# A float32 encoder layer on one core: the seven products of a block unit in another order, the fourth one handed on to the next unit

## The chip, the core and the metric

The kernel runs on one core of a Trainium2 chip. Its engines are TensorE (PE in the profile; PEld is its weight load), VectorE (DVE), ScalarE (ACT), GpSimd (POOL) and SyncE (SP). Here SP issues nearly all transfers and POOL the accumulating ones. The metric is the time of one execution in device microseconds.

## What is computed

One layer of a bidirectional encoder on two sequences that share all weights, x_sample (1024 tokens) and x_prompt (512 tokens), D = 2048, float32 throughout. Cut to its products:

```python
def mixer_layer(x, norm_g, w_in, w_dw, b_dw, ln_g, ln_b, w_pw, sink, w_out):
    h = rms_norm(x, norm_g)
    z = h @ w_in                                   # 2048 x 5632
    c_val, c_glu, c_gate, q, k, v, a_gate = jnp.split(z, split_points, axis=-1)
    ...
    conv_out = conformer_conv(c_val, c_glu, w_dw, b_dw, ln_g, ln_b, w_pw) * jax.nn.silu(c_gate)
    attn_out = banded_sink_attention(q, k, v, sink) * jax.nn.silu(a_gate)
    mix = jnp.concatenate([conv_out, attn_out], axis=-1) @ w_out
    return x + mix
```

A final RMS norm follows. The convolution is a depthwise one of 31 taps (on VectorE), the attention is banded over 128-token blocks.

## The kernel before, in words

**Splitting.** A float32 product is made of three passes. Each operand is split into a high part (a copy that is rounded, on ScalarE, L496) and a low part (the difference, on VectorE, L497), and TensorE adds high x high, high x low and low x high. A weight block so needs a raw buffer ("raw", three of 512 KB) and a split buffer ("hl", three).

**Units.** The sample's product with w_in and w_out is cut into units (`Unit`). A unit takes 8 x 128 rows of the contraction and two column tiles of 128 and all 1024 tokens, as a 2 x 2 block product by Winograd's form of Strassen's method: seven products P1 to P7 where eight would be needed. One product is 4 x 3 matmuls of 128 x 128 weights on 512 tokens. Its weight operands are four blocks and three sums of them:

- P1 uses the first column's upper half, P2 its lower half, P3 the second column's lower half;
- P5 uses second upper minus first upper, P6 second lower minus that, P7 second lower minus second upper, P4 first lower minus P6's operand.

The token operands are four blocks and four sums, split once for all units of a stage. The seven products add up in three PSUM banks: `BANK` puts P1, P6, P7 and P4 into bank 0, P2 into bank 1, P5 and P3 into bank 2; `FRESH` products start their bank. After each product a tap (`tap`, L225, in `Onto` L292) reads the bank, and the next product in that bank, which goes on adding, waits until it has been read. A tap writes a tile from `E()`, which hands out tiles of tag g and u in turn (four of each).

**Weights.** A unit has four preps. `load0` (L122) fetches both halves of the first column, `load1` (L126) of the second. `make0` splits the first raw block (for P1 and P2); `make1` makes three sums (L141) and splits P5's and P6's operand; `make2` makes P7's sum and splits it with the second column's lower half (P7 and P3); `make3` splits P4's operand alone. `OPERAND` says which prep and which half of it a product uses. `product` (L185 on) asks for the block it needs, and after its first three matmuls for those up to `look` (three) ahead; `w_prep_now` makes a block and loads those up to three preps on. A block that two products use leaves its hl buffer after the second. In units with `keep`, low parts are also stored for the prompt, and in those with `sums` the three sums, for the last stage.

**Order.** `ALONE` is the order of the seven products in a unit, `TURNS` that in the first pair of units. The first two units of four of the six unit stages are interleaved product by product (`grouped`), the second one in banks of tags s and pt (`side`). `weights_setup` lines up all preps, `run` goes over items (one unit, a pair of units, or a job). The stages are: a unit of plain products, then 7 units (conv columns, first half of the contraction), 8 units (the same, second half, with `total`), 14 and 14 units (the other columns), jobs (`Job`, matmuls L645) for the prompt's input product and the pointwise products, with the attention between, 16 units of `Onto` for w_out, and the prompt's last product (L1781). The unit stages run from 31.7 to 873 us and from 1560 to 1893 us.

**At the seams.** `switch` loads the token sums of the next stage while the last unit of a stage runs and splits them after given products (`unit.after`). `Onto.begin` loads the tile onto which a product is added, `ahead` products early, and `next` hands this on to the next unit. In the last unit of the sample's input products (`end`), `load_two` fetches the prompt's blocks and `follow(step)` splits four of them after product `step`; `end.look` is one less than elsewhere.

**Who waits where.** Instructions of one engine run in the order in which they were put into its queue; the kernel gives weight preps and taps a higher priority (`URGENT`) than the work of its lanes (convolution, attention, preparation), which is doled out as products go by (`tick`).

Of the kernel before, what the change touches and what calls it, by code (L numbers as in the profile page):

```python
# [47 lines left out]
HALF = 4  # L48
# [44 lines left out]
class Unit:  # L93
# [10 lines left out]
    def __init__(self, e, w, cols, k, part, done=None, keep=None):  # L104
        self.e, self.k, self.part, self.done, self.keep = e, k, part, done, keep
        self.total = done is not None
        self.w = [w[c][:, k : k + 2 * HALF, :] for c in cols]
        self.before, self.after, self.d = [], {}, {}
        self.side = False
        self.order = ALONE  # L110
        self.sums = None


# [5 lines left out]

    def load0(self):  # L120
        self.r1 = self.e.raw_tile()
        self.e.nc.sync.dma_start(self.r1, self.w[0])  # L122

    def load1(self):
        self.r2 = self.raw()
        self.e.nc.sync.dma_start(self.r2, self.w[1])  # L126

    late = False
    look = NHL
    STEPS = range(7)  # L130
    landing = LANDING

    def make0(self):
        t = self.e.hl_tile()
        self.e.parts(t[:, 0], t[:, 1], self.r1)
        if self.keep:
            self.e.store(self.keep[0][:, self.k : self.k + 2 * HALF, :], t[:, 1].bitcast(F32).rearrange("p a b c -> p (a b) c"))
        return t

    def sub(self, out, x, y):  # L140
        self.e.nc.vector.tensor_tensor(out, x, y, ALU.subtract)  # L141

    def make1(self):
# [9 lines left out]
        if self.sums:  # L153
            for name, x in (("P5", r1[:, 0]), ("P6", t2), ("P4", r1[:, 1])):
                self.e.store(self.sums[name], x)
        t = self.e.hl_tile()
        for o, x in enumerate((r1[:, 0], t2)):
            self.e.parts(t[:, 0, o], t[:, 1, o], x)
        return t

    def make2(self):
        self.sub(self.r2[:, 0], self.r2[:, 1], self.r2[:, 0])
        if self.sums:
            self.e.store(self.sums["P7"], self.r2[:, 0])
        t = self.e.hl_tile()
        self.e.parts(t[:, 0], t[:, 1], self.r2)
        self.r2 = None
        if self.keep:
            self.e.store(self.keep[1][:, self.k + HALF : self.k + 2 * HALF, :], t[:, 1, 1].bitcast(F32))
        return t  # L170

    def make3(self):
# [6 lines left out]
    def open(self):  # L179
        e = self.e  # L180
        tags = ("s", "s", "pt") if self.side else ("a", "b", "c")
        self.bank = [None] * 3
        self.tags = tags

    def product(self, step, late):  # L185
        e, nc = self.e, self.e.nc
        name = self.order[step]
        p, o = OPERAND[name]
        i = self.at[p]
        e.w_prep(i + 1)  # L190
        hl = e.hl[i]
        n = BANK[name]
        if name in FRESH:
            self.bank[n] = e.PS(self.tags[n], [W])
        acc = self.bank[n]
        toks = e.T[SUMS[name]]
        for j in range(HALF):
            for q, (l, r) in enumerate(((0, 0), (0, 1), (1, 0))):
                nc.tensor.matmul(  # L199
                    acc,  # L200
                    hl[:, l, o, j, :],
                    toks[j][:, r],
                    start=name in FRESH and j == 0 and q == 0,
                    stop=name in LAST and j == HALF - 1 and q == 2,
                    skip_group_check=True,
                )
# [52 lines left out]
class Onto(Unit):  # L259
# [5 lines left out]

    def __init__(self, e, w, cols, k, source, part, done=None):
        super().__init__(e, w, cols, k, part, done)
        self.source, self.next, self.ahead = source, None, 1

    def begin(self, n):  # L270
        if n not in self.d:
            self.d[n] = self.e.E()
            self.e.nc.sync.dma_start(self.d[n], self.source(*n))

    def open(self):
        super().open()
        self.begin((0, 0))

    def product(self, step, late):
        step_of = step + self.ahead  # L280
        if step_of < len(self.order):
            name = self.order[step_of]
            if name in self.START:
                self.begin(self.START[name])
        elif self.next:
            self.next.begin((0, 0))
        return super().product(step, late)

    def tap(self, name):
# [11 lines left out]
class Plain(Unit):  # L301
# [8 lines left out]
        self.raws = [self.e.raw_tile() for _ in range(2)]  # L310

    def load_some(self, c, k, j0=0, j1=HALF):
        self.e.nc.sync.dma_start(self.raws[c][:, k, j0:j1], self.w[c][:, k * HALF + j0 : k * HALF + j1, :])

    def make_some(self, c, k, j0=0, j1=HALF):
        e = self.e
# [100 lines left out]
class Encoder:  # L417
# [158 lines left out]

    def weights_setup(self, items):
        self.preps = []
        for item in items:
# [37 lines left out]
    def run(self, items):  # L617

        nc = self.nc
        late = []  # L620
        for n, item in enumerate(items):
# [602 lines left out]
class Mix:  # L1224
# [66 lines left out]
    def fill(self):  # L1291
# [4 lines left out]

        def load(step):
            if step < 7:
                held.append(self.load_sum(SUMS[ALONE[step]], 1, True, e.F))

        def put(step):
            for j, x in enumerate(held.popleft()):
                self.token_sum(SUMS[ALONE[step]], 1, j, x)

        load(0)
        load(1)
# [497 lines left out]
def encoder(ctx, tc, a):  # L1804
# [73 lines left out]
    def switch(unit, nxt, g, seq):  # L1878
# [3 lines left out]
        roomy = seq is sample  # L1882

        def load(step):
            held[step] = seq.load_sum(SUMS[ALONE[step]], g, step % 3 or roomy and step == 6)

        def follow(step):
            for j, x in enumerate(held.pop(step)):
                seq.token_sum(SUMS[ALONE[step]], g, j, x)
            if step < 4 - roomy:  # L1890
                load(step + 3)
            elif step == 4 and roomy:
# [137 lines left out]
    chain = over[0] + over[1]  # L2030
    for u, v in zip(chain, chain[1:]):
        u.next = v
    jobs += grouped(over[0], None) + grouped(over[1], e.A)
    for u in over[1][:2]:
        u.ahead = 0
    over[1][0].next = None
    fj[-1].before.append(lambda: chain[0].begin((0, 0)))

    fj = last.first_jobs()
    over[1][-1].after[2] = [lambda: e.prep.add(last.attention_parts())]  # L2040
# [65 lines left out]
```

## Time and profile before

| | |
|---|---|
| median of three runs | 2104.36 us |
| lowest, highest | 2098.03, 2104.57 us |
| profiled execution | 2106.77 us |
| its span, from first to last instruction | 2104.9 us |
| mean granted TensorE clock | 0.997 |

The stages that consist of units, in busy microseconds of each engine (the stretches are us from the span's start):

| stretch | length | PE | DVE | ACT | DMA share |
|---|---|---|---|---|---|
| 31.7 to 170 | 138.30 | 133.85 | 98.05 | 85.73 | 0.88 |
| 170 to 323 | 153.00 | 153.00 | 130.48 | 68.19 | 0.83 |
| 323 to 590 | 267.00 | 266.22 | 243.29 | 116.06 | 0.66 |
| 1565 to 1895 | 330.00 | 324.82 | 293.53 | 144.66 | 0.83 |

How to read it: a matmul's record is longer than the time to the next one (389 ns against some 227), because matmuls are pipelined; a PE that shows busy throughout runs at its pace. A row of a timeline gives the start, the microseconds, the engine, the line, and out<-in by the tiles' names with the number of instructions merged; a bracket holds the idle time ahead of it and what ended it. In a list of waits three numbers follow: microseconds in total, how often, and the longest.

### The profile page before, as it was taken

To read this page: it belongs to the slowest core of one execution; us is meant where nothing else is said; L and a number is where in the kernel's file an instruction comes from. 1 tells how busy PE (TensorE), PEld (TensorE's weight loads), DVE (VectorE), ACT (ScalarE), POOL (GpSimd) and SP (SyncE) were. 2 spreads that over 40 slices of the span, in tenths; PEclk is the share of its full clock that TensorE was granted. 3 is DMA by queue.
4 is the path that set the end of the run, shared out by engine and by line. 5 is a ranking of instruction groups with operands and counts; after the bars stand their busy time and mean duration, and the time that the engine had idled before them with its cause. 6 is when DMAs were issued, how large, how long until landed. Compare 5 with 4: busy or idle time off the path is not lost. (4 is left out here: it accounts for less than half of the span.)

```text
span 2104.9 us, 26942 instructions
## 1 busy us (share of the span) xinstructions
PE 2067.4 (98%) x9250; PEld 1696.0 (81%) x9250; DVE 1751.4 (83%) x2851; ACT 1042.5 (50%) x1685; POOL 77.3 (4%) x92
## 2 busy tenths in 40 slices
PE   9999999999999999999999999999999999999997
PEld 7878888888877887778888888887878788888886
DVE  8758798998889999999556877776799988898876
ACT  6476435333454443544456777336553343455444
POOL 0001110000002111100000000000000000000000
PEclk9999999999999999999999999999999999999999
DMA  7988887865577776955456565996689898678998
GB/s 265 322 290 247 203 217 226 295 201 172 181 228 193 172 170 170 270 162 163 156 170 190 169 187 180 315 332 223 233 276 305 269 321 295 207 251 272 299 323 276
DMA packets 247449, 494.53 MB, mean 235 GB/s; under 512 B 23184, under 2 KB 83984, under 8 KB 247312
## 3 DMA queue, kind: packets, MB, share of 16 engines
q1 hardware_dynamic: 234640, 469.74, 67.4%
q0 software_dynamic: 12672, 23.07, 6.9%
q8 instruction: 72, 1.18, 0.2%
q14 instruction: 65, 0.53, 0.1%
HBM read 331.77 MB, written 160.96 MB: 234 GB/s over the span
## 5 line engine op out<-in xcount | busy, mean ns | idle before, releaser
L199 PE MATMUL a<-t,hl 128*128 128x512 f32 x2640 | 633.4, 390 | 10.0 <-ACT u L225 4.8
L199 PEld LDWEIGHTS a<-t,hl 128*128 128x128 f32 x2640 | 493.2, 188 | 118.4 <-ACT u L225 8.1
L496 ACT ACTIVATE hl<-raw 128x1024 fp32r<-128x1024 f32 (+3 forms) x360 | 324.6, 902 | 435.6 <-DVE raw L141 96.3
L497 DVE TENSOR_TENSOR hl<-raw,hl 128x1024 fp32r<-128x1024 f32 (+3 forms) x360 | 370.1, 1028 | 152.6 <-ACT hl L496 148.7
L645 PE MATMUL a<-t,hl 128*128 128x512 f32 x1344 | 329.4, 395 | 0.5 <-DVE hl L497 0.5
L199 PE MATMUL c<-t,hl 128*128 128x512 f32 x1320 | 320.1, 390 | 3.1 <-DVE u L292 2.0
L199 PEld LDWEIGHTS c<-t,hl 128*128 128x128 f32 x1320 | 247.0, 188 | 56.6 <-DVE u L292 3.4
L645 PEld LDWEIGHTS a<-t,hl 128*128 128x128 f32 x1344 | 249.2, 189 | 51.4 <-DVE hl L497 1.0
L1013 DVE SCALAR_TENSOR_TENSOR f<-f,c_w_dw,f 128x512 f32<-128x512 f32 x248 | 175.3, 748 | 0.3
L645 PE MATMUL c<-t,hl 128*128 128x512 f32 x672 | 165.4, 394 | 0.0
L976 DVE SCALAR_TENSOR_TENSOR f<-f,c_w_dw,f 128x512 f32<-128x512 f32 x232 | 163.7, 746 | 1.8 <-ACT f L971 1.8
L645 PE MATMUL b<-t,hl 128*128 128x512 f32 x672 | 163.4, 392 | 0.2 <-DVE hl L497 0.2
L199 PE MATMUL b<-t,hl 128*128 128x512 f32 x660 | 160.2, 390 | 0.0
L645 PEld LDWEIGHTS b<-t,hl 128*128 128x128 f32 x672 | 124.9, 188 | 25.3 <-DVE hl L497 0.7
L645 PEld LDWEIGHTS c<-t,hl 128*128 128x128 f32 x672 | 125.1, 189 | 24.4
L199 PEld LDWEIGHTS b<-t,hl 128*128 128x128 f32 x660 | 123.7, 188 | 25.5
L1005 DVE SCALAR_TENSOR_TENSOR f<-f,w_both,f 128x512 f32<-128x512 f32 x120 | 89.8, 749 | 1.8
L225 ACT ACTIVATE u<-a 128x512 f32<-128x512 f32 x82 | 48.6, 592 | 56.5 <-PE a L199 53.7
L404 ACT ACTIVATE hl<-raw 128x1024 fp32r<-128x1024 f32 x44 | 46.4, 1056 | 60.5 <-PE a L645 22.3
L225 ACT ACTIVATE g<-a 128x512 f32<-128x512 f32 x78 | 46.3, 593 | 56.3 <-PE a L199 52.7
L1143 ACT ACTIVATE p<-p,tiny 128x384 f32<-128x384 f32 (+1 forms) x96 | 54.6, 570 | 38.4 <-DVE tiny L1140 28.1
L496 ACT ACTIVATE a<-pt 128x512 fp32r<-128x512 f32 x64 | 38.0, 593 | 68.6 <-PE pt L1163 68.2
(333 smaller groups left out, 2575.5 us busy)
## 6 DMA issues: line engine op xcount, KB each, us to landing
raw<-w_in SPq DMA_DIRECT2D x171, 512.0 KB, 5.1
raw<-wsum_P SPq DMA_DIRECT2D x32, 512.0 KB, 5.2
raw<-w_out SPq DMA_DIRECT2D x31, 512.0 KB, 5.4
raw<-w_pw SPq DMA_DIRECT2D x24, 512.0 KB, 4.4
raw<-w_last SPq DMA_DIRECT2D x24, 512.0 KB, 5.2
wsum_P<-raw SPq DMA_DIRECT2D x47, 256.0 KB, 3.5
f<-x_s SPq DMA_DIRECT2D x16, 512.0 KB, 7.2
a<-sum_S SPq DMA_DIRECT2D x24, 256.0 KB, 6.0
```

The source lines that it names most:

```text
L199: nc.tensor.matmul(acc, hl[:, l, o, j, :], toks[j][:, r], start=name in FRESH and j == 0 and q == 0, stop=name in LAST and j == HALF - 1 a ...
L225: nc.scalar.activation(t, bank, AF.Copy)
L404: e.nc.scalar.activation(t[:, 0], raw, AF.Copy)
L496: nc.scalar.activation(hi, x, AF.Copy)
L497: nc.vector.tensor_tensor(lo, x, hi.bitcast(F32), ALU.subtract)
L645: nc.tensor.matmul(job.acc[0], hl[:, l, kk // HALF, kk % HALF, :], r, start=i == 0 and p == 0, stop=i == nk - 1 and p == 2,)
L976: nc.vector.scalar_tensor_tensor(t, h[:, j : j + T], w(j), t, ALU.mult, ALU.add)
L1005: nc.vector.scalar_tensor_tensor(m0, odd[:, j : j + H], both(j), m0, ALU.mult, ALU.add)
L1013: nc.vector.scalar_tensor_tensor(out, d[:, j : j + H], w(2 * j + k), out if j else m0, ALU.mult, ALU.add)
L1143: nc.scalar.activation(p[:, 0:n], p[:, 0:n], AF.Exp, bias=nm[:, h : h + 1], accum_out=l[:, h : h + 1])
```

## The change

The seven weight operands are paired anew: P1 with P5, P6 with P2, P3 with P7, and P4 alone. For this `load0` fetches the upper halves of both columns and `load1` the lower halves, each by two transfers of 256 KB where one of 512 KB was. `make0` makes P5's sum and splits it with P1's block. `make1` makes P6's and P4's operand, splits P6's with the first column's lower half (P2), and then makes P7's sum from P6's operand and the first column's upper half. `make2` has no sum left. The low parts are stored in pieces as they come.

The order of a single unit becomes P1, P5, P6, P2, P3, P7, P4 (`SKEWED`). Where the next item is a unit or a pair of units too, P4 isn't run at the unit's end but behind the next unit's second product (behind the first of both units of a pair), and the prep of its block is put behind the next unit's first prep. Pairs of units, and the last unit ahead of a job, keep their P4 and run P1, P5, P6, P2, P7, P3, P4 (`BESIDE`); the first pair runs P1, P5, P2, P6, P7, P3, P4.

`Onto` starts the load for the next product that `run` has in its list, across units. `switch` follows the new order, with its last two splits behind products 0 and 2 of the next unit. In the last unit of the sample the four groups of the prompt's blocks are split one step later, blocks 8 to 11 are loaded after step 1 and 12 to 15 after step 2 (before: ahead of the unit, and after step 0), and `look` is three there as well.

```diff
-OPERAND = {"P1": (0, 0), "P2": (0, 1), "P6": (1, 1), "P5": (1, 0), "P7": (2, 0), "P3": (2, 1), "P4": (3, 0)}
+OPERAND = {"P1": (0, 0), "P5": (0, 1), "P6": (1, 0), "P2": (1, 1), "P3": (2, 0), "P7": (2, 1), "P4": (3, 0)}
...
-TURNS = ("P1", "P2", "P5", "P6", "P7", "P3", "P4")
+SKEWED = ("P1", "P5", "P6", "P2", "P3", "P7", "P4")
+BESIDE = ("P1", "P5", "P6", "P2", "P7", "P3", "P4")
+TURNS = ("P1", "P5", "P2", "P6", "P7", "P3", "P4")
...
-        self.w = [w[c][:, k : k + 2 * HALF, :] for c in cols]
+        self.w = [[w[c][:, k + h * HALF : k + (h + 1) * HALF, :] for h in range(2)] for c in cols]
...
     def load0(self):
         self.r1 = self.e.raw_tile()
-        self.e.nc.sync.dma_start(self.r1, self.w[0])
+        for c in range(2):
+            self.e.nc.sync.dma_start(self.r1[:, c], self.w[c][0])
 
     def load1(self):
         self.r2 = self.raw()
-        self.e.nc.sync.dma_start(self.r2, self.w[1])
+        for c in range(2):
+            self.e.nc.sync.dma_start(self.r2[:, c], self.w[1 - c][1])
...
+    def make0(self):
+        r1 = self.r1
+        self.sub(r1[:, 1], r1[:, 1], r1[:, 0])
+        self.keep_sum("P5", r1[:, 1])
+        t = self.e.hl_tile()
+        self.e.parts(t[:, 0], t[:, 1], r1)
+        self.keep_low(0, 0, t[:, 1, 0])
+        return t
...
         r1, r2 = self.r1, self.r2
-        self.sub(r1[:, 0], r2[:, 0], r1[:, 0])
-        self.sub(t2, r2[:, 1], r1[:, 0])
-        self.sub(r1[:, 1], r1[:, 1], t2)
...
+        self.sub(t2, r2[:, 0], r1[:, 1])
+        self.sub(r1[:, 1], r2[:, 1], t2)
+        self.keep_sum("P6", t2)
+        self.keep_sum("P4", r1[:, 1])
         t = self.e.hl_tile()
-        for o, x in enumerate((r1[:, 0], t2)):
+        for o, x in enumerate((t2, r2[:, 1])):
             self.e.parts(t[:, 0, o], t[:, 1, o], x)
+        self.keep_low(0, HALF, t[:, 1, 1])
+        self.sub(r2[:, 1], t2, r1[:, 0])
         return t
...
-        if step in (1, 3, 5, 6):
+        self.used[p] += 1
+        if self.used[p] == 2 or p == 3:
             e.hl.pop(i)
...
+        for item, nxt in zip(items, items[1:] + [[None]]):
             if isinstance(item[0], Unit):
                 lists = [u.preps() for u in item]
                 for u in item:
                     u.at = []
+                    u.pending = self.skewed(item) and self.skewed(nxt, True)
+                    if not u.pending and u.order is SKEWED:
+                        u.order = BESIDE
                 for p in range(len(lists[0])):
                     for u, l in zip(item, lists):
-                        u.at.append(len(self.preps))
-                        self.preps.append(l[p])
+                        if p == 3 and u.pending:
+                            continue
+                        put(u, l[p])
+                    if p == 0 and rest:
+                        put(*rest)
+                        rest = None
+                if item[0].pending:
+                    rest = item[0], lists[0][3]
...
+    def skewed(self, item, two=False):
+        return isinstance(item[0], Unit) and not isinstance(item[0], Plain) and (two or len(item) == 1)
...
+            for step in range(steps):
+                for u in item:
+                    if step == 6 and u.pending:
+                        waiting = u
+                    else:
+                        plan.append((item[0], u, step))
+                if waiting and waiting is not item[0] and step == (len(item) == 1):
+                    plan.append((item[0], waiting, 6))
+                    waiting = None
...
-                for step in range(len(item[0].STEPS)):
-                    for u in item:
-                        late = u.product(step, late)
+                while plan and plan[0][0] is item[0]:
+                    _, u, step = plan.popleft()
+                    if plan and isinstance(plan[0][1], Onto) and plan[0][1].ahead:
+                        plan[0][1].begin(plan[0][1].order[plan[0][2]])
+                    late = u.product(step, late)
...
-            u, at = (unit, step + 1) if step < 6 else (nxt, 0)
+            u, at = (unit, step + 1) if step < 5 else (nxt, 2 * (step - 5))
...
-        if step == 0:
-            load_two(12)
-            load_two(14)
+        if step < 2:
+            load_two(8 + 4 * step)
+            load_two(10 + 4 * step)
...
-        for j in range(0, 12, 2):
+        for j in range(0, 8, 2):
             load_two(j)
...
-    end.look = NHL - 1
     end.before.append(last_before)
     for step in range(4):
-        end.after[step] = [lambda step=step: follow(step)]
+        end.after[step + 1] = [lambda step=step: follow(step)]
```

More of the change, by code (lines that the diff above doesn't have):

```diff
@@ L131, with keep_low, keep_sum @@
     landing = LANDING
[L133 to L138, printed above, removed]
     def sub(self, out, x, y):
         self.e.nc.vector.tensor_tensor(out, x, y, ALU.subtract)
+    def keep_low(self, c, k, x):
+        if self.keep:
+            k += self.k
+            self.e.store(self.keep[c][:, k : k + HALF, :], x.bitcast(F32))
+    def keep_sum(self, name, x):
+        if self.sums:
+            self.e.store(self.sums[name], x)
+    def make0(self):
[6 more added lines that the diff above has]
+        return t
     def make1(self):
@@ L167, in make2 @@
         self.r2 = None
-        if self.keep:
-            self.e.store(self.keep[1][:, self.k + HALF : self.k + 2 * HALF, :], t[:, 1, 1].bitcast(F32))
+        self.keep_low(1, HALF, t[:, 1, 0])
         return t
@@ L183, in open @@
         self.tags = tags
+        self.used = [0] * 4
     def product(self, step, late):
@@ L267, in __init__, with begin @@
         super().__init__(e, w, cols, k, part, done)
-        self.source, self.next, self.ahead = source, None, 1
-    def begin(self, n):
-        if n not in self.d:
+        self.source, self.ahead = source, True
+    def begin(self, name):
+        n = self.START.get(name)
+        if n and n not in self.d:
             self.d[n] = self.e.E()
             self.e.nc.sync.dma_start(self.d[n], self.source(*n))
-    def open(self):
-        super().open()
-        self.begin((0, 0))
     def product(self, step, late):
[L280 to L286, printed above, removed]
+        self.begin(self.order[step])
         return super().product(step, late)
@@ L620, in run @@
         late = []
+        waiting = None
+        plan = []
+        for item in items:
+            if not isinstance(item[0], Unit):
+                continue
+            steps = len(item[0].STEPS)
+            for step in range(steps):
[6 more added lines that the diff above has]
+                    plan.append((item[0], waiting, 6))
+                    waiting = None
+        plan = deque(plan)
         for n, item in enumerate(items):
@@ L1884, in load @@
         def load(step):
-            held[step] = seq.load_sum(SUMS[ALONE[step]], g, step % 3 or roomy and step == 6)
+            held[step] = seq.load_sum(SUMS[SKEWED[step]], g, step % 3 or roomy and step == 6)
         def follow(step):
             for j, x in enumerate(held.pop(step)):
-                seq.token_sum(SUMS[ALONE[step]], g, j, x)
+                seq.token_sum(SUMS[SKEWED[step]], g, j, x)
             if step < 4 - roomy:
@@ L2029, in encoder @@
         over[1][-1].after[step] = [lambda i=i: last.split(i) for i in range(4 * step, 4 * step + 4)]
-    chain = over[0] + over[1]
-    for u, v in zip(chain, chain[1:]):
-        u.next = v
     jobs += grouped(over[0], None) + grouped(over[1], e.A)
     for u in over[1][:2]:
-        u.ahead = 0
-    over[1][0].next = None
-    fj[-1].before.append(lambda: chain[0].begin((0, 0)))
+        u.ahead = False
+    fj[-1].before.append(lambda: over[0][0].begin("P1"))
     fj = last.first_jobs()
```

20 lines of the change are left out of this document (9 added, 11 removed).

## The prediction, made before the result was known

> **What bounds the kernel now.** I read the page's head first, then the list of waits for TensorE alone, then the timelines around single waits.
>
> ```profile
> span 2104.9 us, 26942 instructions
> PE 2067.4 (98%) x9250; PEld 1696.0 (81%) x9250; DVE 1751.4 (83%) x2851; ACT 1042.5 (50%) x1685; POOL 77.3 (4%) x92
> ```
>
> PE is busy in 2067.4 of 2104.9 us, and the change takes no matmul away. So the most that any reordering could bring is the idle rest, 37.5 us, and a part of that lies in the start, the end and the attention work. What belongs to the units' line L199 stands in the list of waits (us in total, times, longest):
>
> ```profile
> PE a L199 <- ACT u L225: 4.8, 6, 1.3
> ...
> PE a L199 <- ACT g L225: 2.3, 2, 1.2
> ...
> PE c L199 <- DVE u L292: 2.0, 1, 2.0
> PE a L199 <- DVE hl L497: 1.8, 1, 1.8
> ...
> PE s L199 <- ACT hl L496: 1.1, 1, 1.1
> PE a L199 <- DVE u L292: 1.0, 1, 1.0
> PE c L199 <- ACT g L225: 0.9, 1, 0.9
> PE s L199 <- DVE hl L497: 0.9, 2, 0.5
> ```
>
> Two kinds. Waits for L225 and L292 are waits for a tap: a product adds into a PSUM bank that the tap of an earlier product still has to read. They are 6 + 2 + 1 + 1 + 1 = 11 waits with 4.8 + 2.3 + 2.0 + 1.0 + 0.9 = 11.0 us. Waits for hl are waits for a weight block that isn't split yet: 4 with 1.8 + 1.1 + 0.9 = 3.8 us. What a wait costs beside its idle time is seen in the timeline of PE (start, us, then the instruction; the bracket is the idle time before):
>
> ```profile
> 121.45 2.88 PE L199 MATMUL c<-t,hl 128*128 128x512 f32 x12
> 125.48 5.76 PE L199 MATMUL a<-t,hl 128*128 128x512 f32 x24 [1.15 <-ACT u L225]
> 131.07 2.88 PE L199 MATMUL b<-t,hl 128*128 128x512 f32 x12
> ...
> 834.27 2.88 PE L199 MATMUL b<-t,hl 128*128 128x512 f32 x12
> 838.23 3.03 PE L199 MATMUL a<-t,hl 128*128 128x512 f32 x12 [1.08 <-ACT g L225]
> ...
> 869.76 3.04 PE L199 MATMUL a<-t,hl 128*128 128x512 f32 x12 [1.30 <-ACT u L225]
> ```
>
> ```profile
> 1815.85 2.88 PE L199 MATMUL b<-t,hl 128*128 128x512 f32 x12
> 1818.57 1.07 PE L199 MATMUL c<-t,hl 128*128 128x512 f32 x4
> 1820.61 3.00 PE L199 MATMUL a<-t,hl 128*128 128x512 f32 x12 [0.97 <-DVE u L292]
> ```
>
> Undisturbed, a product of 12 matmuls takes 1818.57 - 1815.85 = 2.72 us, two take 5.44 and a unit of seven 19.04. After the product at 121.45 the next was due at 124.17; it came at 125.48, and the two products from there took 131.07 - 125.48 = 5.59. The loss is 1.31 + 0.15 = 1.46 us for 1.15 of idle time: 0.31 more than the list shows. I add 0.31 to each wait.
>
> Why the tap is late is in ACT's timeline just before:
>
> ```profile
> 123.79 1.06 ACT L873 ACTIVATE f<-f 128x1024 f32<-128x1024 f32 x1 [2.34 <-DMA f<-x_s]
> 124.85 0.58 ACT L225 ACTIVATE u<-a 128x512 f32<-128x512 f32 x1
> ```
>
> The tap stands behind an instruction that waited for a load. The b, a and c of the rows above name the case: a c (P3) then a (P4) at 125.48, b (P2) then a (P6) at 838.23. In the old order every pair on one bank, P1 and P6, P5 and P3, P7 and P4, has exactly one product between (P6 and P7 too), 2.72 us in which the tap must run.
>
> **The order of the products.** In a single unit that hands its P4 on, P1, P5, held P4, P6, P2, P3, P7, P1', P5', P4 puts two products between P1 and P6, P6 and P7, P7 and P4, and three between P5 and P3; P3 and the next P5 have two. Each tap so gets at least 2.72 us more, and the longest wait in the list is 2.0 us. The pairs of units alternate and have three or more between. Only the last unit ahead of a job keeps its P4 (P7, P3, P4), and the wait at 869.76 (1.30) is of that kind: it stays. Term one: 10 waits, 11.0 - 1.3 = 9.7 us, plus 10 x 0.31 = 3.1, makes **-12.8 us**. Its bound on the weak side comes from VectorE in the stage with most of the small waits:
>
> ```profile
> 590.00:873.00 283.00, 275.35 (x1206) 223.51 (x1206) 271.16 (x404) 132.65 (x207) 48.18 (x55) 1.00 0.74 192
> ```
>
> PE idles 283.00 - 275.35 = 7.65 us here, DVE only 11.84. Of PE's, 1.3 stays, and 1.8 and 1.1 + 0.5 are waits for hl; 2.95 is left for taps, in about five waits of the size of the one at 838.23 or less: 2.95 + 5 x 0.31 = 4.5. If DVE's backlog ate all of it, the term would be -8.3.
>
> **The weight blocks.** The subtractions stay four a unit at 0.686 us each, as do the splits:
>
> ```profile
> L141 DVE TENSOR_TENSOR raw<-raw,raw 128x512 f32<-128x512 f32 x55 | 37.8, 686 | 0.6
> ```
>
> With three hl buffers, a block is made once the block three before it has been used up, while the two in between are used. Now the four blocks get 3, 3, 4 and 4 products (8.16, 8.16, 10.88, 10.88 us). In the new sequence (first block, held fourth, second, third) they get 4, 4, 3 and 3. The first gains a subtraction and 2.72 us; the third loses both. The second, the heaviest (three subtractions and two half splits, 5 x 0.686 = 3.4 us on DVE), keeps 8.16 us. Work hidden in 8.16 stays hidden: zero, with -5.0 as the low bound (all four hl waits, 3.8 + 4 x 0.31) and the second rival as the high one.
>
> **The loads.** Steady units around 400 us show how early they go out (DVE, SP's issues, then ACT):
>
> ```profile
> 404.99 1.22 DVE L497 TENSOR_TENSOR hl<-raw,hl 128x1024 fp32r<-128x1024 f32 x1
> 409.25 0.68 DVE L497 TENSOR_TENSOR hl<-raw,hl 128x512 fp32r<-128x512 f32 x1
> 417.98 0.68 DVE L141 TENSOR_TENSOR raw<-raw,raw 128x512 f32<-128x512 f32 x1
> ```
>
> ```profile
> 406.64 0.38 SPq L126 DMA_DIRECT2D raw<-w_in  x1
> 409.96 0.33 SPq L122 DMA_DIRECT2D raw<-w_in  x1
> ```
>
> ```profile
> 431.92 1.05 ACT L496 ACTIVATE hl<-raw 128x1024 fp32r<-128x1024 f32 x1
> ```
>
> The second load (L126) leaves when the third block's split (404.99 + 1.22) frees a raw buffer and is first read at 417.98, 11.3 us later. The first load of the unit after next (L122) leaves behind the fourth block's split (409.25 + 0.68) and is read at 431.92, 22.0 us later. Holding the fourth block shortens the latter: its split moves to P3 and the reader to the next unit's P6, five products on, 13.6 us less the split's delay, some 12. The former becomes about 10: the third block is made at the held P4, and the reader starts at P1', five products (13.6) later, less some 3.5 for the split (1.05 on ACT, 1.22 on DVE and one or two instructions in the queues). Against that:
>
> ```profile
> L122 SPq DMA_DIRECT2D raw<-w_in x43: 327/333/551, 16.6 to 821.1; - x43
> ...
> DMA to landing us min/median/max: 4.0/5.6/7.7
> ```
>
> ```profile
> u<-xT_s SPq DMA_DIRECT2D x16, 256.0 KB, 4.9
> ```
>
> A load of 512 KB lands in 7.7 us at worst; a load of 256 KB typically in 4.9. Two halves side by side, with one more issue of 0.33 us on SP, land within 8.0 and stay hidden behind the 10 to 12 us of matmuls. The 59 units (7 + 8 + 14 + 14 + 16 by the code, 43 of them on w_in) so issue 118 loads more, and 22 units (those that keep low parts) store them in three pieces where they took two: 140 x 0.33 = 46 us of SP over the whole span, off the path: zero. What queues behind a blocked issue on SP are the stores of parts and the next raw loads. Were the cover gone, each unit would lose what the landing exceeds it by.
>
> [...]
>
> **The last unit of the sample.** Its loads of the prompt's blocks 12 to 15 are asked for after step 2 and used after step 4; so far after steps 0 and 3. The cover shrinks from three products to two.
>
> ```profile
> 868.50 0.72 ACT L499 ACTIVATE t<-a,c_norm_g 128x512 fp32r<-128x512 f32 x1 [1.67 <-DMA a<-xr_d]
> ```
>
> ACT already stands 1.67 us for such a load, just ahead of the tap that PE waits for at 869.76. One product less may add up to 2.72; the splits also move a product nearer to the first job. I take half, **+1.4**, with 0 and +4 (2.72 plus one wait of 1.30) as bounds.
>
> **The tap's tiles.** The tiles that taps write (four g, four u) live longer: P1's now until P2 at step 3, not 1, P5's until P7 three products later. One shortage is in the trace:
>
> ```profile
> 671.26 0.60 ACT L225 ACTIVATE g<-c 128x512 f32<-128x512 f32 x1 [3.60 <-DMA v_d<-g]
> ```
>
> Behind that tap on ACT queue other taps and hl splits; PE lost 0.9 + 0.31. I charge one more such loss, **+1.3** with its start, and take 0 and +3.6 as bounds.
>
> **The sum.** -12.8 + 1.4 + 1.3 = -10.1 us. The profiled execution took 2106.77 us (span 2104.9 and 1.9 around it) and becomes 2096.7. It lies 2.4 above the median of the runs shown, 2104.36, so for a median I say **2094**; its own range is 2089 (-15.1, the hl waits gone too) to 2099 (-8.3 + 2.7 = -5.6).
>
> **Rivals.** *The wait only changes its name* (2101). ACT stays blocked by the same late loads, and hl splits stand in the same queue; moreover PE's order on the chip isn't quite the program's: at 1818.57 four matmuls of P5 stand ahead of P6. The new order may be broken up alike elsewhere, so that the change doesn't do what it says. With the first term at its weak bound and the second charge at its upper one: -8.3 + 4 + 1.3 = -3.0. Against it: a split has 8.16 us, and ACT's holds seen here are 1.7 to 3.6.
>
> *Blocks late, slower* (2114). Place: 590 to 873, where DVE is 96% busy. There the third block loses 2.72 us of lead and stands behind the second, the heaviest, in DVE's queue. A late block costs 1.8 + 0.31 = 2.1 us (the hl wait in the list). Some 14 units run there; the gain of 10.1 is gone at five late blocks, and nine or ten give +20 - 10.1 = +10. For it: the hl wait of 1.8 lies in this stretch. Against it: the total of DVE's work is unchanged, and the first block, so far in 8.16 us, has more room.
>
> *The halves late* (2126): if the two halves landed 12 us after their issue, 2 over the cover, the 16 output units would lose 32: +32 - 10.1 = +22. No landing over 7.7 speaks for it.
>
> **The numbers.** Forecast 0.56; a larger gain (all taps, all hl waits, no charges: -12.8 - 5.0 = -17.8, so 2087, and down to 2081 if some of the attention's waits between products go too), 0.08; renamed wait 0.16; late blocks 0.16; late halves 0.04. The range 2081 to 2111 leaves out most of the last two and little below. About 0.3%, 6.3 us, is what a measurement of this kernel can tell from no change. Of the forecast's 0.56 all but 0.06 lies below 2098.0; with the larger gain and a little of the renamed wait, faster 0.6. Same, 2098 to 2110.7, takes the rest of these and the small end of the late blocks: 0.22. Slower: 0.18.
>
> **What would show it.** Right: the waits of L199 for L225 and L292 shrink from 11 to one to three, P4 stands between c and a of the next unit, and L199's loss before 873 us falls by about 10. Term by term: a longer hold by xr_d near 870 for the second; ACT waits for g or u to be stored for the third. Wrong: more waits for hl, above all between 590 and 873; raw landing above 10 us; taps still waited for in single units.

## The result, and the profile after

| | median | lowest, highest | runs |
|---|---|---|---|
| before | 2102.98 us | 2098.03, 2107.57 | 6 |
| after | 2212.56 us | 2206.47, 2216.51 | 6 |

The ratio is 1.0522 with a 95% interval of [1.0498, 1.0546]: some 110 us slower, outside the predicted range (2081 to 2111). The profiled execution of after took 2216.46 us. Head of its page, and the stage whose row of before the prediction shows (columns: length, then busy us of PE, PEld, DVE, ACT and POOL, the granted TensorE clock, DMA share, GB/s):

```profile
span 2214.7 us, 27179 instructions
PE 2103.9 (95%) x9250; PEld 1707.0 (77%) x9250; DVE 1755.2 (79%) x2851; ACT 1035.3 (47%) x1685; POOL 76.9 (3%) x92
```

```profile
590.00:873.00 283.00, 253.57 (x1065) 200.10 (x1064) 234.01 (x347) 111.39 (x177) 33.09 (x38) 0.98 0.63 167
```

TensorE's idle time grew from 37.5 to 2214.7 - 2103.9 = 110.8 us, and the same 9250 matmuls are busy 36.5 us longer (2103.9 - 2067.4), at a lower clock (0.985 on the mean, where it was 0.997). Work has hardly grown anywhere (DVE 1755.2 after 1751.4). PE idles for lines of VectorE and ScalarE. In the list of waits the units' matmuls (now L212) wait for adds (L259), taps (L239) and splits (L502):

```profile
PE c L212 <- DVE g L259: 12.4, 8, 3.0
PE c L212 <- DVE u L259: 11.8, 9, 2.6
PE a L212 <- DVE hl L502: 11.7, 12, 3.5
...
PE a L212 <- ACT u L239: 10.5, 3, 5.8
```

What these adds and splits stood behind is seen in the view of the sums' line (now L138): what VectorE idled for ahead of a sum.

```profile
  DMA raw<-w_in: 156.9, 78
  DMA raw<-w_out: 28.4, 19
```

That makes 185.3 us of VectorE waiting for raw loads; before, all 55 sums of the group quoted in the prediction had 0.6 us of idle time in front of them. Two sums wait, as VectorE's list of waits shows: block one's, whose output is called raw (second upper minus first upper), and block two's first, called p, or a and g in the later stages, by the tile it goes into. (Of the 93.0 us for raw, 6.3 belong to the sum right behind p, P4's operand, which waits for the other half of the same load.)

```profile
DVE raw L138 <- DMA raw<-w_in: 93.0, 44, 5.3
DVE p L138 <- DMA raw<-w_in: 63.9, 34, 5.1
```

Were the loads slow? The view of the second load's line (L130) gives the times from issue to landing:

```profile
DMA to landing us min/median/max: 3.1/4.7/7.0
```

No: the median is 4.7 us, where the old 512 KB load of L122 took 5.6, and the maximum is 7.0 where it was 7.7. The sums come too early. One case from load to matmul, in the timelines of SP, VectorE and TensorE:

```profile
313.55 1.39 SPq L130 DMA_DIRECT2D raw<-w_in  x2
...
321.95 0.81 SPq L125 DMA_DIRECT2D raw<-w_in  x2
```

```profile
319.38 0.69 DVE L138 TENSOR_TENSOR p<-raw,raw 128x512 f32<-128x512 f32 x1 [2.60 <-DMA raw<-w_in]
...
320.65 0.68 DVE L259 TENSOR_TENSOR g<-b,g 128x512 f32<-128x512 f32 x1
321.25 0.68 DVE L502 TENSOR_TENSOR hl<-raw,hl 128x512 fp32r<-128x512 f32 x1
...
323.11 0.68 DVE L259 TENSOR_TENSOR u<-c,u 128x512 f32<-128x512 f32 x1
...
327.86 0.69 DVE L138 TENSOR_TENSOR raw<-raw 128x512 f32<-128x512 f32 x1 [2.15 <-DMA raw<-w_in]
```

```profile
323.85 4.61 PE L212 MATMUL c<-t,hl 128*128 128x512 f32 x12 [2.63 <-DVE u L259]
328.29 5.62 PE L212 MATMUL a<-t,hl 128*128 128x512 f32 x24
```

The load leaves at 313.55; the sum is at the head of VectorE's queue at 319.38 - 2.60 = 316.78, 3.2 us later, when it hasn't landed. Two adds and a low split that have nothing to do with the load stand behind it in VectorE's queue and start only after it, at 320.65, 321.25 and 323.11. The add at 323.11 is what the next product in bank c waits for: TensorE idles 2.63 us, and its next 12 matmuls take 328.29 - 323.85 = 4.44 us instead of 2.72. A wait of 2.60 us on VectorE so stood ahead of a loss of 2.63 + 1.72 = 4.35 us on TensorE. The next load, the first one of the unit after (321.95), goes the same way: block one's sum is due at 327.86 - 2.15 = 325.71, 3.8 us behind it.

**Theory S**, which the experiments test: in the new pairs the first sums of blocks one and two need nothing but their load (block two's also block one's sum, which is made a block earlier), so the order worked out at build time puts them where it takes the load to have landed. (What that order assumes of a landing is not read off anywhere; the traces show only where the sums stand.) Before, the one sum that reads a fresh load overwrote block one's raw half, so it had to come after block one's split, far behind its load. Rivals: the halves as such (H), the held block's longer hold on a raw buffer (N), loads that go out too late for the new pairs wherever the sums stand (L).

### The profile page after: what moved, and what is told of

Same layout as the page of the kernel before. It is cut to its first block, busy times and chain, and to the rows that moved or that the text cites. A ratio compares the mean times of both kernels' runs of the same rounds, so it can differ in the third digit from the quotient of the medians.

```text
span 2214.7 us, 27179 instructions
## 1 busy us (share of the span) xinstructions
PE 2103.9 (95%) x9250; PEld 1707.0 (77%) x9250; DVE 1755.2 (79%) x2851; ACT 1035.3 (47%) x1685; POOL 76.9 (3%) x92
## 4 chain that ended last, share of the span: by engine, by line
PE 39%; DMA 26%; DVE 24%; issue 5%; ACT 3%; SPq 1%; DVEq 0%; ACTq 0%
DMA raw<-w_in 12%; PE a L686 11%; DVE hl L502 7%; PE c L686 5%; PE a L212 5%; PE b L686 5%; PE c L212 3%; DMA raw<-w_out 3%; DVE f L1054 2%; DVE raw L138 2%; PE pv L1199 2%; PE s L1170 2%; DVE t L502 2%; PE b L212 2%; PE pt L1204 1%
## 5 line engine op out<-in xcount | busy, mean ns | idle before, releaser
L212 PE MATMUL a<-t,hl 128*128 128x512 f32 x2640 | 642.4, 396 | 37.9 <-DVE hl L502 11.7
L212 PEld LDWEIGHTS a<-t,hl 128*128 128x128 f32 x2640 | 499.7, 191 | 155.7 <-DVE hl L502 19.0
L502 DVE TENSOR_TENSOR hl<-raw,hl 128x1024 fp32r<-128x1024 f32 (+3 forms) x356 | 366.5, 1030 | 98.3 <-ACT hl L501 97.0
L212 PE MATMUL c<-t,hl 128*128 128x512 f32 x1320 | 331.7, 398 | 29.4 <-DVE g L259 12.4
L686 PE MATMUL a<-t,hl 128*128 128x512 f32 x1344 | 331.6, 396 | 0.5 <-DVE hl L502 0.5
L212 PEld LDWEIGHTS c<-t,hl 128*128 128x128 f32 x1320 | 249.5, 191 | 94.3 <-DVE g L259 16.5
L686 PEld LDWEIGHTS a<-t,hl 128*128 128x128 f32 x1344 | 250.7, 190 | 51.4 <-DVE hl L502 1.4
L686 PE MATMUL c<-t,hl 128*128 128x512 f32 x672 | 166.1, 394 | 0.0
L212 PE MATMUL b<-t,hl 128*128 128x512 f32 x660 | 160.0, 389 | 0.0
L212 PEld LDWEIGHTS b<-t,hl 128*128 128x128 f32 x660 | 124.2, 188 | 26.0
L138 DVE TENSOR_TENSOR raw<-raw 128x512 f32<-128x512 f32 x59 | 40.7, 690 | 103.1 <-DMA raw<-w_in 86.7
L239 ACT ACTIVATE u<-a 128x512 f32<-128x512 f32 x82 | 48.5, 591 | 111.2 <-PE a L212 85.0
L239 ACT ACTIVATE g<-a 128x512 f32<-128x512 f32 x78 | 46.1, 591 | 91.4 <-PE a L212 70.5
L138 DVE TENSOR_TENSOR p<-raw,raw 128x512 f32<-128x512 f32 x40 | 27.6, 691 | 63.9 <-DMA raw<-w_in 63.9
```

Of the source, the lines that this page charges most:

```text
L212: nc.tensor.matmul(acc, hl[:, l, o, j, :], toks[j][:, r], start=name in FRESH and j == 0 and q == 0, stop=name in LAST and j == HALF - 1 a ...
L239: nc.scalar.activation(t, bank, AF.Copy)
L502: nc.vector.tensor_tensor(lo, x, hi.bitcast(F32), ALU.subtract)
L686: nc.tensor.matmul(job.acc[0], hl[:, l, kk // HALF, kk % HALF, :], r, start=i == 0 and p == 0, stop=i == nk - 1 and p == 2,)
```

## The experiments

Ratios are to the kernel before, run beside each, with 95% intervals.

**1. The old kernel with each load in halves.**

```diff
-        self.e.nc.sync.dma_start(self.r1, self.w[0])
+        for h in range(2):
+            self.e.nc.sync.dma_start(self.r1[:, h], self.w[0][:, h * HALF : (h + 1) * HALF, :])
```

(`load1` alike.)

> The kernel before, with old pairs and old order, each raw load as two transfers of 256 KB. Theory S (the first sums of blocks one and two are put on VectorE as soon as the schedule thinks their load has landed, since in the new pairing they wait for nothing else): halves alone cost nothing, 2097 to 2112 us, VectorE waits for raw loads below 10 us. Rival H (halves as such, by their issue, landing or the schedule's idea of them): at least 30 us slower, 2135 to 2210, with the waits of VectorE or ScalarE for raw loads above 60 us.

2101.32 us, ratio 1.0006 [0.9992, 1.0019]; in VectorE's list of waits a single sum waits for a load, 1.4 us. With the old order halves cost nothing that can be measured.

**2. The changed kernel with whole loads.** One transfer takes both columns; block halves are addressed by a flag, as the lower-numbered column comes first.

```diff
-        for c in range(2):
-            self.e.nc.sync.dma_start(self.r1[:, c], self.w[c][0])
+        self.e.nc.sync.dma_start(self.r1, self.both[0])
...
-        for c in range(2):
-            self.e.nc.sync.dma_start(self.r2[:, c], self.w[1 - c][1])
+        self.e.nc.sync.dma_start(self.r2, self.both[1])
```

> The changed kernel with each raw load as one transfer of 512 KB over two columns, all else as changed. Theory S: 2190 to 2225 us, VectorE still waits 130 us or more for raw loads in front of the sums. Rival H (halves): 2090 to 2120, waits below 30 us.

2214.74 us, ratio 1.0540 [1.0524, 1.0556]. Its waits (sums at L142):

```profile
DVE p L142 <- DMA raw<-w_in: 75.9, 34, 6.4
DVE raw L142 <- DMA raw<-w_in: 73.7, 37, 5.9
```

The waits are much the same without halves. H falls.

**3. The changed kernel without the hold.**

```diff
-                    u.pending = self.skewed(item) and self.skewed(nxt, True)
+                    u.pending = False
```

> The changed kernel without the hold: every unit finishes its own seventh product, pairs and halves as changed. Theory S: the sums still have nothing but the load to wait for, so 2150 to 2220 us with more than 100 us of VectorE waits for raw loads. Rival N (the held block keeps its raw buffer and so delays the loads): 2090 to 2125 us, waits below 30 us.

2197.06 us, ratio 1.0461 [1.0433, 1.0490], and these waits:

```profile
DVE p L138 <- DMA raw<-w_in: 69.3, 26, 6.5
DVE raw L138 <- DMA raw<-w_in: 55.2, 26, 6.6
```

The new pairs alone do most of the harm, so N isn't needed for it.

**4. The two sums in turn.** `parts` notes its last low split, and each of the two sums is issued on VectorE behind the split noted last. This is an edge of order alone; loads, buffers and products are as in the change.

```diff
             nc.vector.tensor_tensor(lo, x, hi.bitcast(F32), ALU.subtract)
+            self.split = nc.cur_bb.bb.instructions[-1]
...
-        self.sub(r1[:, 1], r1[:, 1], r1[:, 0])
+        with self.e.tc.issue_after(self.e.split):
+            self.sub(r1[:, 1], r1[:, 1], r1[:, 0])
...
-        self.sub(t2, r2[:, 0], r1[:, 1])
+        with self.e.tc.issue_after(self.e.split):
+            self.sub(t2, r2[:, 0], r1[:, 1])
```

> The changed kernel with two ordering edges a unit: the first sum of block one and the first sum of block two are issued on VectorE behind the low split of the block made just before. Theory S: VectorE's waits for raw loads fall from some 190 us to below 70 and the time to 2100 to 2140 us. Rival L (the loads themselves go out too late for the new pairs, wherever the sums stand): the waits stay above 120 us, the hl waits of TensorE too, and the time stays at 2180 to 2220 us.

2105.45 us, ratio 1.0020 [1.0003, 1.0037]. Head, VectorE's waits for raw loads ahead of sums, and PE's waits on the units' line (L214; taps L241 and L299):

```profile
span 2098.9 us, 27207 instructions
PE 2065.4 (98%) x9250; PEld 1695.6 (81%) x9250; DVE 1755.1 (84%) x2851; ACT 1039.5 (50%) x1685; POOL 76.9 (4%) x92
```

```profile
DVE p L138 <- DMA raw<-w_in: 1.6, 4, 0.6
...
DVE raw L138 <- DMA raw<-w_in: 1.0, 1, 1.0
```

```profile
PE a L214 <- ACT u L241: 3.7, 3, 2.2
PE c L214 <- DVE tiny L1193: 3.0, 1, 3.0
...
PE a L214 <- ACT hl L504: 2.1, 2, 1.2
...
PE a L214 <- ACT g L241: 1.2, 2, 0.9
...
PE a L214 <- DVE u L299: 0.9, 1, 0.9
...
PE s L214 <- DVE hl L505: 0.2, 1, 0.2
```

185.3 us of waits become 2.6, and the loss of 5.2% becomes 0.2%. PE's idle time is back at 2098.9 - 2065.4 = 33.5 us, its busy time at 2065.4. With the same loads, TensorE waits only 2.1 + 0.2 us for splits (hl): the loads were in time for them all along, and L falls. The row for L1193 is taken up below.

**5 and 6. One of the two edges each.**

> The changed kernel with the ordering edge on the first sum of block one alone; the sum of block two is free as in the change. Theory S: that sum's waits for its load stay (60 to 95 us in all on VectorE), block one's go; each sum does its share, 2130 to 2180 us. Rival O (one of the two sums does nearly all the harm): below 2115 us here and above 2190 with the other edge alone, or the reverse.

> The changed kernel with the ordering edge on the first sum of block two alone; block one's sum is free. Theory S: block one's waits stay (80 to 120 us on VectorE), block two's go; 2140 to 2190 us. Rival O: near 2105 or near 2210, with the other edge alone at the other end.

2138.95 us, ratio 1.0185 [1.0156, 1.0214], with block two's sum free; 2158.34 us, ratio 1.0287 [1.0265, 1.0309], with block one's free. The row of the sum that was left free, in the fifth and the sixth:

```profile
DVE p L138 <- DMA raw<-w_in: 45.9, 24, 5.9
```

```profile
DVE raw L138 <- DMA raw<-w_in: 89.7, 42, 6.2
```

Beyond the 1.0020 with both edges, block two's sum costs 1.0185 - 1.0020 = 1.65% and block one's 2.67%, some 35 and 56 us: each does its share, and together they cost a little more than the two added up.

**7. Both edges, no hold** (the edits of 3 and 4).

> Both ordering edges and no hold of the fourth block's product. Theory G (two products between instead of one spare some ten waits of taps, as the prediction's first term says, some 8 to 13 us): 2112 to 2122 us, and more waits of TensorE for the taps' lines than with the hold. Rival Z (the hold is worth nothing that can be measured): 2098 to 2109 us.

2117.62 us, ratio 1.0092 [1.0068, 1.0117]. The time is as G said, the reason isn't (TensorE's waits again):

```profile
PE s L214 <- ACT hl L504: 7.6, 4, 3.0
...
PE a L214 <- ACT g L241: 2.3, 3, 1.1
PE a L214 <- ACT hl L504: 2.0, 2, 1.1
PE a L214 <- ACT u L241: 1.6, 4, 0.7
PE a L214 <- DVE u L299: 1.4, 2, 1.0
...
PE a L214 <- DVE hl L505: 1.2, 2, 0.7
...
PE s L214 <- DVE hl L505: 0.4, 1, 0.4
```

Taps are waited for no longer than with the hold (2.3 + 1.6 + 1.4 = 5.3 us here and 0.3 in a row not shown, 3.7 + 1.2 + 0.9 = 5.8 there). What the hold saves is waits for weight blocks: 7.6 + 2.0 + 1.2 + 0.4 = 11.2 us here, 2.1 + 0.2 in the fourth experiment. The two edges are worth 1.0461 - 1.0092 = 3.7% without the hold and 5.0% with it, so the early sums cost somewhat more under the hold.

**8. The old kernel with its first sum freed.** In the 43 units on w_in the sum goes into a tile of its own and no longer waits for block one's split.

```diff
-        self.sub(r1[:, 0], r2[:, 0], r1[:, 0])
-        self.sub(t2, r2[:, 1], r1[:, 0])
+        t1 = r1[:, 0] if self.late else self.e.PT("p", NP, [HALF, P])
+        self.sub(t1, r2[:, 0], r1[:, 0])
+        self.sub(t2, r2[:, 1], t1)
```

> The kernel before with one thing altered: in the 43 units on w_in the first sum goes into a tile of its own, so that it no longer waits until block one's split has read the buffer that it overwrote; order, pairs and loads are the old ones. Theory S: the schedule puts it right behind its load's landing as it counts it, VectorE waits 30 to 90 us for raw loads that it did not wait for before, and the time goes to 2115 to 2165 us. Rival P (the new pairs or the new order do the harm, not the freed sum): 2096 to 2108 us, waits below 10 us.

2108.74 us, ratio 1.0059 [1.0039, 1.0079], and a row that the kernel before doesn't have:

```profile
DVE p L141 <- DMA raw<-w_in: 40.8, 29, 3.3
```

So the mechanism exists without the change's order, pairs or halves. By the waits, which are in the range expected for S, P falls; the time is a miss for both, just above P's range and below that of S: 40.8 us of waits in this row cost 0.59%, some 12 us; the fifth's 45.9 cost some 35. So the length of the waits alone doesn't set the price. That it goes by what stands behind the waiting sum is the author's reading of single cases and was not tried by itself.

**9. The hold with the old pairs and loads.** Order P1, P2, held P4, P6, P5, P7, P3; makes and loads as before.

> The old pairs, old loads and old sums (each sum sheltered behind block one's split), with the hold of the fourth block's product alone: P1, P2, the held P4, P6, P5, P7, P3. Theory S: the hold does no harm by itself, 2085 to 2108 us, VectorE waits for raw loads below 10 us; were its spacing of the a bank worth what the prediction said, 3 of its 5 to 10 us would show (2088 to 2096). Rival N (the hold takes a raw buffer away for too long): above 2115 us, with waits for raw loads above 30.

2137.95 us, ratio 1.0173 [1.0151, 1.0195]: a miss for S as stated. Its VectorE waits for raw loads again (sums at L136, loads at L128; the list of waits first, then one case in VectorE's and SP's timelines):

```profile
DVE raw L136 <- DMA raw<-w_in: 75.0, 32, 5.5
```

```profile
394.75 1.22 DVE L501 TENSOR_TENSOR hl<-raw,hl 128x1024 fp32r<-128x1024 f32 x1
397.75 1.22 DVE L501 TENSOR_TENSOR hl<-raw,hl 128x1024 fp32r<-128x1024 f32 x1
401.83 0.69 DVE L136 TENSOR_TENSOR raw<-raw,raw 128x512 f32<-128x512 f32 x1 [1.53 <-DMA raw<-w_in]
```

```profile
396.40 0.38 SPq L128 DMA_DIRECT2D raw<-w_in  x1
```

The third block's split ends at 395.97 and lets the load out at 396.40. With the hold, block one's split follows at once (397.75), because the fourth block's prep has moved behind it. The sum is still sheltered, but the shelter now ends 2.6 us behind the load (398.97), and the sum is due at 400.30, 3.9 us behind it, where the prediction read off 11.3 for the kernel before.

**10. The fourth experiment with whole loads** (the edits of 2 and 4).

> The changed kernel with both ordering edges and each load whole again (512 KB over two columns), so 118 issues fewer. Theory S: halves cost nothing, 2098 to 2110 us, as with the halves (2105). Rival Q (the halves' issues on SP hold back the stores and with them the taps' tiles, which is what is left of the loss): 2085 to 2097 us.

2106.12 us, ratio 1.0021 [1.0008, 1.0034]. Q falls: the 118 issues more are not what is left of the loss.

**11. The changed kernel with its two sums on GpSimd**, without edges.

```diff
-        self.sub(r1[:, 1], r1[:, 1], r1[:, 0])
+        self.e.nc.gpsimd.tensor_tensor(r1[:, 1], r1[:, 1], r1[:, 0], ALU.subtract)
```

(Block two's first sum alike.)

> The changed kernel with its two first sums a unit on GpSimd, without ordering edges, so that what waits for the loads is another queue than VectorE's. Theory S (it is VectorE's order, taps and splits behind a waiting sum, that costs): VectorE's waits for raw loads vanish, GpSimd stands in them instead, and the time falls by 60 us or more, to 2100 to 2150 us, as GpSimd's sum is longer than VectorE's 0.69 us and may itself be late. Rival L (the splits need the sums that early, whoever makes them): above 2180 us.

2204.73 us, ratio 1.0506 [1.0471, 1.0541]: a miss. The sum that makes P4's operand still stands on VectorE and waits there for GpSimd, whose sums take 1.34 us (L165) and 1.64 us (L151) on average where VectorE's take some 0.69, and for another 34.2 us for raw loads:

```profile
DVE raw L138 <- POOL p L165: 52.9, 20, 5.7
```

The wait only moved one instruction on. The time is in the range given for L, but with a wait still at VectorE this run doesn't tell S from L; the fourth does.

**12. The ninth with an edge**: the first sum of block two behind the split noted last, which is the held block's.

> The old pairs with the hold (as in the run before, 2138 us), and one ordering edge: the first sum of block two goes on VectorE behind the low split of the block made before it, which with the hold is the held fourth. Theory S: the hold's harm was that block one's split, the old shelter, now stands right behind the third block's, some 3 us after the load left; with the edge the waits for raw loads fall below 10 us and the time to 2092 to 2106 us. Rival W (the hold with old pairs is slow for its spacing of taps and blocks): the time stays above 2120 us with the waits gone.

2104.65 us, ratio 1.0017 [1.0002, 1.0032], with 4.7 + 2.6 us of waits of sums for raw loads; W falls. With the old pairs, too, the hold does its harm through the place of the sum, not through a buffer (N) or the spacing of products.

**13. The fourth once more.**

> The changed kernel with both ordering edges once more, for its median and a second profile. Theory R (the prediction's gain of some 10 us from taps is there in the profiled execution and is lost in others by chance of timing): a median of 2092 to 2100 us here. Rival K (the gain in taps is real but small and paid for by the last unit's loads and the attention stage): 2100 to 2110 us again, with waits of TensorE in units below those of the kernel before and those elsewhere above.

2104.70 us, ratio 1.0017 [1.0004, 1.0031]. Its profile (span 2100.0 us) has 6.2 + 1.3 + 0.4 = 7.9 us of waits that are named after taps, below the 11.0 of before, a wait of 4.0 us for the attention's work, and the row for L1193 again:

```profile
PE c L214 <- DVE tiny L1193: 3.3, 1, 3.3
```

R falls: the median shows no gain. K's range holds; whether there is a gain in taps at all is taken up below. No version beat the kernel before.

## Why the prediction was wrong, point by point

**The loads: the step that failed.** The prediction took the reader of the second load to be bound to its block's split, "five products (13.6) later, less some 3.5", and so gave it about 10 us. Its reader is the block's first sum, which holds no hl buffer and follows no product. It gave the first load "some 12" by the same reasoning, and there the reader is block one's sum. In the old pairs that sum overwrote half of a raw block which the split of block one still had to read; the 11.3 us that the prediction read off at 417.98 were owed to this one dependence, which the prediction didn't name; where experiment 8 takes it away, the sum waits for its load 29 times. The new pairs drop it twice (the sum of block two goes into a fresh tile, and block one gains a sum that reads nothing but its load), and the hold shortens it where it is kept (experiment 9). The leads in the case shown were 3.2 and 3.8 us, where 10 and 12 were counted on, against a median landing of 4.7. Priced at zero, the step was worth 5.0% (1.0522 against 1.0020).

**The rival that came nearest** was "the halves late" (2126, chance 0.04): right that a raw load would not be there, wrong in what moves. It looked for landings above 10 us; the median landing was 4.7 (L130) and 4.8 (L125), the latest 7.0 and 9.0, and the readers came sooner. Its price was off too: 2 us in 16 units, where VectorE stood 185.3 us.

**What a wait costs.** The prediction added 0.31 us to each wait of TensorE. In the case at 323.85, 1.72 us came on top of an idle time of 2.63, because the granted clock was 0.50 for some 3.4 us behind it (324.15 to 327.55; the last section shows the row), in which TensorE by that clock does the work of 1.7; over the span PE's busy time rose by 36.5 us beside 73.3 us more of idle time.

**The weight blocks.** "Work hidden in 8.16 stays hidden" counted durations only. The sums' 0.69 us were hidden; the place of the first one in VectorE's queue wasn't looked at. With the sums in turn the term is right in sign: waits for hl fall from 3.8 us to 2.3, and experiment 7 puts most of the hold's worth here.

**Term one**, -12.8 us, can be read off where the sums are in turn. Waits that are named after taps fall from 11 with 11.0 us to 6 with 5.8 (experiment 4) or 7.9 (13). But the old order has only 9 with 8.5 us in experiment 1's profile, and one wait has merely changed its name. The row for L1193, 3.0 us in experiment 4, 2.9 in 10 and 3.3 in 13, is one wait of a product that goes on adding in bank c. VectorE's timeline in experiment 4, then TensorE's:

```profile
1637.16 0.69 DVE L299 TENSOR_TENSOR u<-c,u 128x512 f32<-128x512 f32 x1 [2.02 <-DMA u<-xT_s]
1637.77 0.17 DVE L1193 RECIPROCAL tiny<-tiny 128x4 f32<-128x4 f32 x1
```

```profile
1638.00 1.16 PE L214 MATMUL c<-t,hl 128*128 128x512 f32 x4 [2.95 <-DVE tiny L1193]
```

The tap of bank c stood 2.02 us for the tile that it adds to, and L1193 is the instruction right behind it in VectorE's queue. With this wait the taps cost 8.8 us in experiment 4 and 11.2 in 13, against 11.0 and 8.5 in the two profiles of the old order: no gain is shown, and the term came to about nothing. That is what the rival "the wait only changes its name" described. Nor does a comparison without the hold show that two products between spare the taps (5.6 us, experiment 7).

**The last unit of the sample**, +1.4: right in kind. In the fourth experiment ScalarE's hold for xr_d (ahead of 857.13) is 3.97 us where it was 1.67, and the wait for the tap behind it (at 859.52) 2.20 where it was 1.30. The jobs that follow wait 2.0 + 0.5 us for splits where it was 0.5 + 0.2.

**The tap's tiles**, +1.3, were not tried by themselves.

**The sum.** With the failed step mended, the rest of the change comes to +0.2% and not to the predicted -10.1 us, so the forecast would have been missed without it too: term one, its largest, was not there. The two profiled executions of that kernel have spans (2098.9 and 2100.0 us) below the 2104.9 of the old one, while both medians lie above; but the old order's other profile (experiment 1) has 2095.7. What makes up the +0.2% stays open.

## What to carry to other kernels

When an edit changes which buffer an instruction writes or reads, ask what that instruction now waits for, not only how long it takes: a dependence that looks like a cost may be what keeps it behind a load. Where others stand behind it in the queue, as two adds and a split stood behind the sum that waited 2.60 us, an instruction that needs nothing but a transfer belongs behind work that is certain to end later than the landing, by an edge of order if no data forces it. And read the lead of a load as the time to its first reader, then name what holds that reader there. When a wait leaves a list, look for it under the name of the instruction that stands behind its old cause.

## What the runs showed of the hardware

The granted clock fell by half after single gaps in TensorE's work, but the length of the gap alone did not decide it. In the changed kernel TensorE waited 5.90 us ahead of 407.31, 2.63 us ahead of 323.85 (the case above) and 3.21 us ahead of 1889.30. The rows of the first and the last follow, then the stretches behind all three, which show the clock (the number before the DMA share):

```profile
407.31 0.80 PE L758 MATMUL s<-u,ones_r 128*128 128x512 f32 x1 [5.90 <-DVE u L753]
...
1889.30 3.00 PE L212 MATMUL a<-t,hl 128*128 128x512 f32 x12 [3.21 <-DVE g L297]
```

```profile
407.30:413.00 5.70, 5.69 (x14) 4.50 (x15) 4.74 (x10) 0.60 (x1) 0.00 (x0) 0.51 0.89 294
413.00:424.00 11.00, 11.00 (x50) 9.13 (x49) 9.30 (x14) 5.33 (x8) 0.00 (x0) 1.00 0.49 181
```

```profile
324.20:327.40 3.20, 3.20 (x9) 2.50 (x8) 1.52 (x3) 1.11 (x2) 0.86 (x1) 0.50 1.00 235
1889.30:1895.00 5.70, 5.70 (x25) 4.72 (x26) 3.66 (x6) 0.00 (x0) 0.00 (x0) 1.00 0.87 278
```

For 5.70 us behind the longest gap the clock is 0.51 on the mean, then it is 1.00. Behind the gap of 2.63 us it is 0.50 for some 3.4 us (324.15 to 327.55), and behind that of 3.21 us it stays at 1.00. So the clock was halved behind 2.63 us and not behind 3.21. What decides it, these three cases don't show.
